# Ragged self-attention on one core: another order of the work ahead of the loops

## The chip, the cores and the metric

The kernel runs on one core of one Trainium2 chip. The metric is the device time of one execution in microseconds (us), taken as the median of several runs. Times inside an execution are counted from the start of the profiled span.

## What is computed

For each of 32 batch entries `b`, the first `lengths[b]` rows of `x[b]` (up to 512 rows of 512 numbers) are projected to queries, keys and values by `w_qkv`, split into 8 heads of 64, and attention is computed within those rows. The other rows of the output are zero.

```
qkv = x_b @ w_qkv;  q, k, v = split(qkv)        # x_b: (seq_len, 512)
scores = q @ k.T / sqrt(64)                     # per head
out_b = softmax(scores) @ v                     # rows past seq_len stay zero
```

`x` is (32, 512, 512) in fp32, `w_qkv` (512, 1536) in fp32; the lengths are drawn between 64 and 511.

## The kernel before, in words

The kernel computes in f16 and accumulates in fp32. It sorts the 32 entries by length on the chip, longest first, and then runs twelve loops (`LOOPS`, L202), one for each width from 512 down to 96. One pass of a loop handles two entries ("positions" 0 and 1). How often each loop runs depends on the lengths: the loop ends are counted on the chip into the tile `ends_i` and are read from there into registers of each of the five engines.

The order of the instructions on each engine is written out by hand. In a loop it stands in the strings of `ORDER` (L204): `S` is a pair of score matmuls with the exponential on ACT (L981, L995), `Q`, `K`, `V` project a part of the *next* entry (matmuls at L228 and L239, copies from PSUM at L1023 and L1039), `A` multiplies by the values and divides (L1065 to L1086), `X` transposes the next input by DMA. So while one entry's attention is computed, the next entry is projected, and the entry after it is loaded and cast. Semaphore waits are worked out by `plan_waits` from what each step reads and writes; they don't change the order.

The change is in `before_loops` (L296), the part ahead of the first loop. It is a list of steps; each engine executes its own steps in the order of that list. In the kernel before it goes like this:

- SP starts the loads of `lengths` (`row`) and of the value weights `w_v` in two halves (L342, L343), ACT starts `col`. POOL makes indices and constants, among them `ones` (L352), 32 partitions by 128.
- DVE makes a sort key for each entry, `least` (L399) is the smallest key, which names the longest entry. Ranks come from comparisons, and two matmuls on PE (`phit_i` and `phit_l`, L446) spread the sorted order and lengths over all partitions (`order`, `slen`).
- SP waits for `least` (`n0`, L538), and then starts the load of the longest entry `x0` in four tiles x0.0 to x0.3 (L540), the query and key weights `w_q` and `w_k` in two halves each (L541 to L544), and, once the order is read (`n1`), `x1` in two halves (L546). All of them are on SP's queue.
- PE runs `warm` (L551), 24 matmuls of the identity that nothing reads, behind the two matmuls of the sort.
- DVE works out the loop ends: `more`, `counts`, `shifted`, `ends_f`, `ends` (L555 to L592), and then casts x0.0 to f16.
- ACT casts the four parts of `w_v` (`shorten`, L679), then x0.1; DVE casts x0.0 and x0.2, POOL x0.3 (`cast_tile`). `turn` (L640) transposes a cast tile on PE (L645) and copies it to `xT0` (L654): below, t00 to t03 are the transposes of x0 and T00 to T03 their copies. `step` (L661) projects: V0 to V3 with `values` (L239), Q0 to Q3 and K0 to K3 with `project` (L228), each followed by a copy from its PSUM bank (L677) on DVE or ACT.
- `read_ends` (L594) loads the three words of `ends_i` into registers of one engine (three loads at L600, with shifts and masks behind each, L606 and L607). DVE does it behind the copy of V2, ACT behind that of V3, POOL and PE amid the query and key steps, SP at the end.
- x1 is cast in four tiles (POOL, DVE, POOL, ACT), and its four transposes stand on PE between K2 and K3. K0 writes PSUM bank 1, which Q2 used before it; K1 writes bank 2, K2 bank 0, the transposes of x1 banks 3 to 6, K3 bank 7.
- Behind that stand the cast of the third entry on POOL (`C`), the first DMA transposes, and empty steps (`joinPE` and others, L815), which make an engine wait for what it needs before the loops.

A program prints the functions that the diff touches, and what calls them, with the line numbers of the profile:

Of the kernel before, what the change touches and what calls it, by code (L numbers as in the profile page):

```python
# [14 lines left out]
ALU = mybir.AluOpType  # L15
AX = mybir.AxisListType

P = 128
# [130 lines left out]
def kernel(  # L149
# [8 lines left out]
    nc = tc.nc  # L158
    B, MAXS, D = x.shape
    NT = MAXS // P  # L160
# [9 lines left out]
    w_q = const.tile([P, NC, D], FP32)  # L170
    w_k = const.tile([P, NC, D], FP32)
# [121 lines left out]
    def of(handles, e):  # L293
        return next(h for h in handles.handles if h.engine == EN[e].engine)

    def before_loops():  # L296
# [35 lines left out]
        def weights(name, tile_, m0, c0, c1):  # L332
            op(
                f"{name}{c0}",
                "SP",
                lambda: sp.dma_start(out=tile_[:, c0:c1, :], in_=w_in[:, c0:c1, m0 : m0 + D]),
                (),
                [f"{name}.{c}" for c in range(c0, c1)],
                dma=True,
            )  # L340
# [11 lines left out]
        ones16 = small("ones", "POOL", lambda t: pool.memset(t, 1.0), shape=(B, P), dtype=F16)  # L352
        limits = small("limits", "POOL", iota([[-32, COUNTS], [0, B // 2]], 0, 448), (), (P, COUNTS, B // 2), I32)
        blank = small("blank", "POOL", lambda t: pool.memset(t, 0.0), shape=(P, P))
        ident = small(
            "ident",
            "POOL",
# [156 lines left out]
            op(name, "SP", load, ("order",))  # L514

        def fetch(name, b, at, k, t0, t1):
            op(
                name,
                "SP",
                lambda: sp.dma_start(  # L520
                    out=x_bufs[b][:, t0:t1, :],
                    in_=xv[bass.ds(found[at][k], 1), :, t0:t1, :].rearrange("o p t d -> (o p) t d"),
                ),
                (),
                [f"xn{b}", *(f"xn{b}.{t}" for t in range(t0, t1))]
                if t1 - t0 == NT
                else [f"xn{b}.{t}" for t in range(t0, t1)],
                dma=True,
            )

        def longest():
            first = nc.alloc_registers("first", engines=[mybir.EngineType.SP])
            reg = of(first, "SP")
            sp.reg_load(reg, least[0:1, 0:1])
            sp.reg_alu(reg, reg, B - 1, op=ALU.bitwise_and)
            found[0] = [nc.snap(first, min_val=0, max_val=B - 1, donate=True)]
# [12 lines left out]
        def warm():  # L549
            for k in range(WARM):  # L550
                nc.tensor.matmul(banks[3][:, 0:P], ident16, ident16, start=True, stop=True)  # L551

        op("warm", "PE", warm, ("ident16",), ("bk3",))

        more = small(  # L555
            "more",
            "DVE",
            lambda t: dve.tensor_tensor(
                out=t,
                in0=slen.rearrange("p (j two) -> p j two", two=2)[:, :, 0]  # L560
                .unsqueeze(1)
                .broadcast_to([P, COUNTS, B // 2]),
                in1=limits,
                op=ALU.is_gt,
            ),
            ("slen", "limits"),
            (P, COUNTS, B // 2),
        )
        counts = small(
            "counts",  # L570
            "DVE",
            lambda t: dve.tensor_reduce(out=t, in_=more, axis=AX.X, op=ALU.add),
            ("more",),
            (P, COUNTS),
        )
        shifted = small(
            "shifted",
            "DVE",
            lambda t: dve.tensor_tensor(out=t, in0=counts, in1=shifts, op=ALU.mult),
            ("counts", "shifts"),  # L580
            (P, COUNTS),
        )
        ends_f = small(
            "ends_f",
            "DVE",
            lambda t: dve.tensor_reduce(
                out=t, in_=shifted.rearrange("p (g k) -> p g k", k=4), axis=AX.X, op=ALU.add
            ),
            ("shifted",),
            (P, COUNTS // 4),  # L590
        )
        op("ends", "DVE", lambda: dve.tensor_copy(out=ends_i, in_=ends_f), ("ends_f",), ("ends",))  # L592

        def read_ends(e, part=None):  # L594
            def load():
                eng = EN[e]
# [82 lines left out]
        for c in range(NC):  # L679
            shorten("wv", w_v, 2 * D, c, "ACT")  # L680

        cast_tile(0, 0, "DVE")
        def joined(name, low, high, bits, after, out=None):

# [12 lines left out]
        def twos(source):  # L697
# [6 lines left out]
        turn(0, 0, "bk4", "DVE")  # L704
        turn(0, 1, "bk5", "ACT")
        cast_tile(0, 2, "DVE")
        cast_tile(0, 3, "POOL")
        step("V0", "bk0", "DVE")
        turn(0, 2, "bk6", "DVE")
        shorten("wq", w_q, 0, 0, "ACT")  # L710
        step("V1", "bk1", "DVE")
        turn(0, 3, "bk3", "ACT")
        shorten("wq", w_q, 0, 1, "POOL")
        op(
            "alive",
            "DVE",
# [19 lines left out]
            (P, B // 2),  # L736
        )
        joined("table", four, computed, 20, ("four", "computed"), table)
        step("V2", "bk4", "DVE")
        shorten("wq", w_q, 0, 2, "ACT")  # L740
        op(
            "M",
            "DVE",
# [24 lines left out]
        shorten("wk", w_k, D, 2, "POOL")  # L768
# [24 lines left out]
        read_ends("SP")  # L793


# [16 lines left out]
        fetch("LD1", 0, 1, 3, 0, NT)  # L812


        op("joinPE", "PE", lambda: None, [f"xT1.{t}" for t in range(NT)], [f"bk{k}" for k in range(3, 7)])  # L815
# [549 lines left out]
```

## Time and profile before

| | |
|---|---|
| median of 3 runs | 345.8 us (345.48, 345.8, 346.64) |
| the profiled execution | 345.26 us |
| its span in the profile | 343.4 us |
| granted TensorE clock, mean | 0.992 |
| first score matmul of the first loop | 22.73 us after the start of the span |

The span is the part of the execution that the profile shows; 1.9 us of the profiled execution lie around it. PE is TensorE with its matmuls, PEld its weight loads, DVE is VectorE, ACT ScalarE, POOL GpSimd, SP SyncE; a q behind a name (SPq, ACTq) means an instruction of the engine's sequencer, such as the start of a DMA or a load of a register, which is not counted as busy time. In the lines of the timeline the columns are start, duration, engine, line, operation, what it writes and reads, and the count; in brackets stands how long the engine had been idle before, and what ended that.

### The profile page before, as it was taken

The numbers are of one execution on the slowest core, as the hardware profiler recorded it, in microseconds if no ns is written. First come the engines' busy times: TensorE is split into PE (matmuls) and PEld (weight loads), VectorE is DVE, ScalarE is ACT, GpSimd is POOL, SyncE is SP. The second block draws the span as 40 slices with busy tenths as digits, with TensorE's granted clock in tenths as the row PEclk, the third lists the DMA queues.
The fourth block names the chain that finished last, engine by engine and source line by source line (L and its number), as shares of the span: only waits on it lengthen the run. The fifth ranks groups of instructions, "written<-read, shape, count | busy, mean of one in ns | idle before, by whom it ended". The sixth has DMA issues, their size and how long they took to land.

```text
span 343.4 us, 10664 instructions
## 1 busy us (share of the span) xinstructions
PE 326.6 (95%) x3846; PEld 201.4 (59%) x3846; DVE 215.3 (63%) x657; ACT 262.7 (77%) x410; POOL 97.9 (29%) x124
## 2 busy tenths in 40 slices
PE   4999999999999999999999999999999999999971
PEld 3444545464555555556655656675677776777751
DVE  6556666667667565465555566677775547777664
ACT  4369899797877878889888898777567788678741
POOL 5466040404030330331133033113222342242311
PEclk9999999999999999999999999999999999999996
DMA  6975974483638936957849549869986656669742
GB/s 224 369 239 131 334 170 135 146 282 90 223 67 287 304 83 226 283 177 285 271 139 307 195 152 338 248 241 238 266 244 198 171 168 216 207 171 238 229 142 79
DMA packets 76060, 73.07 MB, mean 213 GB/s; under 512 B 45808, under 2 KB 45808, under 8 KB 76016
## 3 DMA queue, kind: packets, MB, share of 16 engines
q1 hardware_dynamic: 75968, 72.51, 72.4%
q8 instruction: 24, 0.39, 0.5%
q14 instruction: 20, 0.16, 0.2%
q10 hardware_dynamic: 48, 0.00, 0.0%
HBM read 28.32 MB, written 33.55 MB: 180 GB/s over the span
## 4 chain that ended last, share of the span: by engine, by line
PE 89%; DVE 3%; DMA 2%; issue 1%; SPq 1%; ACT 1%; DVEq 1%; POOL 0%; POOLq 0%
PE banks L228 36%; PE banks L239 21%; PE banks L1065 17%; PE banks L981 15%; DMA out_dram<-out_nat 1%; DVE out_nat L1086 1%; DMA x_nat<-in_x_dram 1%; SPq L255 1%; DVE rcp L1078 1%; DVE qz L677 1%; PE banks L645 1%; DVE v_aug L1039 0%; DVEq L600 0%; DVE rcp L1075 0%; DVE v_aug L677 0%
## 5 line engine op out<-in xcount | busy, mean ns | idle before, releaser
L995 ACT ACTIVATE et<-banks 128x704 f16<-128x704 f32 (+6 forms) x264 | 195.9, 813 | 37.6 <-PE banks L981 36.5
L285 POOL TENSOR_TENSOR x<-x_nat,mask 128x512 f16<-128x512 f32 x87 | 88.3, 1039 | 233.6 <-DVE mask L874 218.3
L228 PE MATMUL banks<-xT,w_r 128*128 128x352 f16 (+11 forms) x1024 | 146.5, 288 | 1.5 <-ACT qz L1023 0.6
L228 PEld LDWEIGHTS banks<-xT,w_r 128*128 128x128 f16 x1024 | 85.0, 98 | 41.6 <-issue 8.7
L239 PE MATMUL banks<-w_r,xT 128*128 128x512 f16 x332 | 85.2, 382 | 0.4 <-ACT xT L654 0.2
L1065 PEld LDWEIGHTS banks<-v_aug,et 128*128 128x128 f16 x1792 | 66.2, 98 | 22.6 <-issue 7.7
L1065 PE MATMUL banks<-v_aug,et 128*128 128x65 f16 x1792 | 74.3, 194 | 1.0 <-ACT et L995 0.7
L1086 DVE TENSOR_TENSOR out_nat<-banks,rcp 128x256 f32<-128x256 f32 (+1 forms) x136 | 64.1, 472 | 5.9 <-DMA out_dram<-out_nat 1.3
L981 PE MATMUL banks<-qz,kT 64*128 64x352 f16 (+11 forms) x640 | 61.6, 298 | 2.8 <-DVE out_nat L1086 1.8
L1075 DVE RECIPROCAL rcp<-banks 128x4 f32<-128x4 f32 (+1 forms) x136 | 25.1, 185 | 44.4 <-PE banks L1065 43.2
L1039 DVE CAST v_aug<-banks 128x512 f16<-128x512 f32 x58 | 40.1, 692 | 18.4 <-PE banks L239 18.2
L239 PEld LDWEIGHTS banks<-w_r,xT 128*128 128x128 f16 x332 | 28.3, 98 | 30.9 <-issue 4.6
L981 PEld LDWEIGHTS banks<-qz,kT 64*128 64x128 f16 x640 | 23.1, 94 | 34.0 <-issue 26.0
L1023 DVE CAST qz<-banks 128x352 f16<-128x352 f32 (+4 forms) x39 | 22.8, 586 | 27.4 <-PE banks L228 27.4
L1023 ACT CAST kT<-banks 128x352 f16<-128x352 f32 (+4 forms) x55 | 26.8, 488 | 13.7 <-PE banks L228 12.8
L1078 DVE TENSOR_TENSOR rcp<-rcp,v_aug 128x4 f32<-128x4 f32 (+1 forms) x136 | 26.1, 192 | 4.7
L1023 ACT CAST qz<-banks 128x320 f16<-128x320 f32 (+5 forms) x52 | 24.5, 477 | 4.9 <-PE banks L228 3.6
L1023 DVE CAST kT<-banks 128x320 f16<-128x320 f32 (+4 forms) x36 | 19.9, 556 | 8.2 <-PE banks L228 7.3
L1039 ACT CAST v_aug<-banks 128x512 f16<-128x512 f32 x21 | 12.5, 596 | 6.1 <-PE banks L239 5.8
L874 DVE TENSOR_SCALAR mask<-alive 128x4 f32 x32 | 5.9, 184 | 5.9 <-issue 5.9
L950 DVE TENSOR_SCALAR v_aug<-alive 128x24 f16 (+3 forms) x32 | 7.2, 224 | 0.0
L446 PE MATMUL banks<-h_hit_i,h_ones 32*128 32x32 f16 x1 | 0.2, 203 | 4.7 <-DVE h_hit_i L429 4.7
(68 smaller groups left out, 48.9 us busy)
## 6 DMA issues: line engine op xcount, KB each, us to landing
x_nat<-in_x_dram SPq DMA_DIRECT2D x12, 768.0 KB, 5.6
out_dram<-out_nat SPq DMA_DIRECT2D x12, 768.0 KB, 4.0
x_nat<-in_x_dram SPq DMA_DIRECT2D x14, 512.0 KB, 4.0
x_nat<-in_x_dram SPq DMA_DIRECT2D x7, 1024.0 KB, 6.7
out_dram<-zeros SPq DMA_DIRECT2D x12, 512.0 KB, 5.4
out_dram<-out_nat SPq DMA_DIRECT2D x12, 512.0 KB, 3.0
out_dram<-out_nat SPq DMA_DIRECT2D x4, 1024.0 KB, 4.7
out_dram<-zeros SPq DMA_DIRECT2D x12, 256.0 KB, 5.4
```

The lines of the kernel that those rows point to most:

```text
L228: last = nc.tensor.matmul(dst[:, 0:N], w_r[:, c, w0 : w0 + P], xT[:, c, 0:N], start=(c == 0), stop=(c == NC - 1),)
L239: last = nc.tensor.matmul(pv, xT[:, c, t * P : (t + 1) * P], w_r[:, c, 2 * D : 3 * D], start=(c == 0), stop=(c == NC - 1),)
L285: return engine.tensor_tensor(out=x16, in0=x32, in1=live.broadcast_to([P, D]), op=ALU.mult)
L950: return nc.vector.tensor_scalar(out=v_bufs[o][:, 0:n, :, HD], in0=alive[:, bass.ds(at("DVE") + (j + 1), 1), 0:n] .rearrange("p o t -> p ( ...
L981: last = nc.tensor.matmul(psc[par][:, x * n128 : x * n128 + N], kT[r, i, kt * P : (kt + 1) * P], qz[r, i, 0:N], start=True, stop=True,)
L995: return nc.scalar.activation(out=et[:, :, x0:x1, 0:N], in_=got.rearrange("p j (x q) -> p j x q", q=n128)[:, :, x0:x1, 0:N], func=AF.Exp, ...
L1023: return copy_on(act)(out=buf[:, ms, 0:N], in_=bank[:, 0 : gm * N].rearrange("p (m q) -> p m q", q=N),)
L1039: return copy_on(act)(out=v_bufs[o][:, t, :, 0:HD], in_=bank.rearrange("p (h d) -> p h d", d=HD))
L1065: last = nc.tensor.matmul(pav[:, g, qt, :], e_bufs[e][:, c0 + qt * P : c0 + (qt + 1) * P], v_aug[:, kt, h, :], start=(kt == 0), stop=(kt = ...
L1075: return nc.vector.reciprocal(out=rcp, in_=pav[:, :, :, HD])
L1078: return nc.vector.tensor_tensor(out=rcp, in0=rcp, in1=v_aug[:, 0:n, h0 : h0 + heads, HD].rearrange("p t g -> p g t"), op=ALU.mult,)
L1086: return nc.vector.tensor_tensor(out=o_t[:, 0:n, h0 * HD : (h0 + heads) * HD].rearrange("p t (g d) -> p g t d", d=HD), in0=pav[:, :, :, 0:HD],
```

## The change

All of it is in `before_loops`; the loops are the same, line for line.

- x0.1 and x0.3 are started by ACT, which first waits for `least` and reads the entry's number itself (`n0a`); x0.0 and x0.2 stay on SP's queue. Nine increments of the semaphore `passed` (`spaced`) stand ahead of that on ACT. ACT's load of its function table, which stood behind the start of `col`, now stands behind these two DMAs.
- `warm0`, 24 matmuls of `ones` by itself (32 partitions, 128 by 128), stands on PE ahead of the two matmuls of the sort. `warm` stays.
- On DVE `shifted`, `ends_f` and `ends` move from ahead of the cast of x0.0 to behind the cast of x0.2; `more` and `counts` stay ahead of it.
- The reads of the three words are spread. ACT reads two of them behind T01 and ahead of its casts of `w_q`, the third behind the copy of V3. DVE reads one behind the copy of V2, one behind Q0's and one behind Q2's; PE one behind each of Q1, Q2 and Q3; POOL one ahead of its casts of `w_q`, one behind, one behind its casts of `w_k`.
- The copy of Q1 goes from DVE to ACT, that of K3 from ACT to DVE. x1 is cast by DVE, ACT, POOL, DVE. POOL casts part 1 of `w_k` ahead of part 2.
- K0 writes bank 3, K1 bank 4, K2 bank 5, K3 bank 7 as before; the transposes of x1 write banks 0, 1, 2 and 6. They stand on PE between K1 and K2, in the order of tiles 0, 1, 3, 2.

```diff
+        def spaced(e, count):
+            def pad():
+                for _ in range(count):
+                    EN[e].sem_inc(passed, 1)
+            op(f"spaced{e}{len(ops)}", e, pad)
...
+        spaced("ACT", 9)
         weights("wv", w_v, 2 * D, 0, NC // 2)
...
+        op(
+            "warm0",
+            "PE",
+            lambda: [
+                nc.tensor.matmul(banks[3][:, 0:P], ones16, ones16, start=True, stop=True)
+                for _ in range(WARM)
+            ][-1],
+            ("ones",),
+            ("bk3",),
+        )
...
         def fetch(name, b, at, k, t0, t1):
+            queue = "ACT" if at == "ACT" else "SP"
             op(
                 name,
-                "SP",
-                lambda: sp.dma_start(
+                queue,
+                lambda: EN[queue].dma_start(
...
-        op("n0", "SP", longest, ("least",))
+        op("n0", "SP", lambda: longest("SP", 0), ("least",))
+        op("n0a", "ACT", lambda: longest("ACT", "ACT"), ("least",))
         for t in range(NT):
-            fetch(f"x0.{t}", 0, 0, 0, t, t + 1)
+            fetch(f"x0.{t}", 0, "ACT" if t % 2 else 0, 0, t, t + 1)
...
         turn(0, 0, "bk4", "DVE")
         turn(0, 1, "bk5", "ACT")
         cast_tile(0, 2, "DVE")
+        shifted = small(
+        ends_f = small(
+        op("ends", "DVE", lambda: dve.tensor_copy(out=ends_i, in_=ends_f), ("ends_f",), ("ends",))
         cast_tile(0, 3, "POOL")
         step("V0", "bk0", "DVE")
         turn(0, 2, "bk6", "DVE")
+        step("V1", "bk1", "DVE")
+        read_ends("ACT", 0)
+        read_ends("ACT", 1)
         shorten("wq", w_q, 0, 0, "ACT")
-        step("V1", "bk1", "DVE")
         turn(0, 3, "bk3", "ACT")
+        shorten("wq", w_q, 0, 2, "ACT")
+        read_ends("POOL", 0)
         shorten("wq", w_q, 0, 1, "POOL")
+        shorten("wq", w_q, 0, 3, "POOL")
+        read_ends("POOL", 1)
+        step("V2", "bk4", "DVE")
+        read_ends("DVE", 0)
...
-        read_ends("DVE")
         step("V3", "bk5", "ACT")
-        read_ends("ACT")
-        shorten("wq", w_q, 0, 3, "POOL")
+        read_ends("ACT", 2)
...
         step("Q0", "bk2", "DVE")
         fetch("x2", 0, 1, 1, 0, NT)
-        shorten("wk", w_k, D, 1, "POOL")
-        step("Q1", "bk0", "DVE")
+        read_ends("DVE", 1)
+        step("Q1", "bk0", "ACT")
         read_ends("PE", 0)
+        shorten("wk", w_k, D, 2, "POOL")
         shorten("wk", w_k, D, 3, "ACT")
         step("Q2", "bk1", "DVE")
-        read_ends("POOL")
-        cast_tile(1, 0, "POOL")
+        read_ends("PE", 1)
+        read_ends("DVE", 2)
+        read_ends("POOL", 2)
+        step("Q3", "bk6", "ACT")
+        read_ends("PE", 2)
+        cast_tile(1, 0, "DVE")
+        cast_tile(1, 1, "ACT")
         cast_tile(1, 2, "POOL")
-        step("Q3", "bk6", "ACT")
-        read_ends("PE", 1)
-        read_ends("PE", 2)
-        cast_tile(1, 1, "DVE")
-        step("K0", "bk1", "DVE")
-        cast_tile(1, 3, "ACT")
-        step("K1", "bk2", "ACT")
-        step("K2", "bk0", "DVE")
-        for t, (bank, eng) in enumerate(
-            (("bk3", "DVE"), ("bk4", "ACT"), ("bk5", "DVE"), ("bk6", "ACT"))
-        ):
+        cast_tile(1, 3, "DVE")
+        step("K0", "bk3", "DVE")
+        step("K1", "bk4", "ACT")
+        for t, bank, eng in ((0, "bk0", "DVE"), (1, "bk1", "ACT"), (3, "bk2", "ACT"), (2, "bk6", "DVE")):
             turn(1, t, bank, eng)
-        step("K3", "bk7", "ACT")
+        step("K2", "bk5", "DVE")
+        step("K3", "bk7", "DVE")
         read_ends("SP")
```

More of the change, by code (lines that the diff above doesn't have):

```diff
@@ L553, in before_loops @@
         op("warm", "PE", warm, ("ident16",), ("bk3",))
[L555 to L592, printed above, removed]
         def read_ends(e, part=None):
@@ L680, in before_loops @@
             shorten("wv", w_v, 2 * D, c, "ACT")
+        more = small(
+            "more",
+            "DVE",
+            lambda t: dve.tensor_tensor(
+                out=t,
+                in0=slen.rearrange("p (j two) -> p j two", two=2)[:, :, 0]
+                .unsqueeze(1)
+                .broadcast_to([P, COUNTS, B // 2]),
+                in1=limits,
+                op=ALU.is_gt,
+            ),
+            ("slen", "limits"),
+            (P, COUNTS, B // 2),
+        )
+        counts = small(
+            "counts",
+            "DVE",
+            lambda t: dve.tensor_reduce(out=t, in_=more, axis=AX.X, op=ALU.add),
+            ("more",),
+            (P, COUNTS),
+        )
         cast_tile(0, 0, "DVE")
@@ L706, in before_loops @@
         cast_tile(0, 2, "DVE")
+        shifted = small(
+            "shifted",
+            "DVE",
+            lambda t: dve.tensor_tensor(out=t, in0=counts, in1=shifts, op=ALU.mult),
+            ("counts", "shifts"),
+            (P, COUNTS),
+        )
+        ends_f = small(
+            "ends_f",
+            "DVE",
+            lambda t: dve.tensor_reduce(
+                out=t, in_=shifted.rearrange("p (g k) -> p g k", k=4), axis=AX.X, op=ALU.add
+            ),
+            ("shifted",),
+            (P, COUNTS // 4),
+        )
+        op("ends", "DVE", lambda: dve.tensor_copy(out=ends_i, in_=ends_f), ("ends_f",), ("ends",))
         cast_tile(0, 3, "POOL")
@@ L812, in before_loops @@
         fetch("LD1", 0, 1, 3, 0, NT)
-        op("joinPE", "PE", lambda: None, [f"xT1.{t}" for t in range(NT)], [f"bk{k}" for k in range(3, 7)])
+        op("joinPE", "PE", lambda: None, [f"xT1.{t}" for t in range(NT)], [f"bk{k}" for k in (0, 1, 2, 6)])
         op("joinACT", "ACT", lambda: None, [f"et{e}" for e in range(4)])
```

16 lines of the change are left out of this document (7 added, 9 removed).

## The prediction

> **What bounds the kernel now.** I read the page first: busy time, and the chain of work that ended last.
>
> ```profile
> PE 326.6 (95%) x3846; PEld 201.4 (59%) x3846; DVE 215.3 (63%) x657; ACT 262.7 (77%) x410; POOL 97.9 (29%) x124
> ...
> PE 89%; DVE 3%; DMA 2%; issue 1%; SPq 1%; ACT 1%; DVEq 1%; POOL 0%; POOLq 0%
> ```
>
> PE carries the chain nearly everywhere, and the loops are the same before and after. So the change is worth as much as it moves the start of the first loop. The second view is PE's timeline ahead of it.
>
> ```profile
> 5.08 2.74 PE L551 MATMUL banks<-h_ident 128*128 128x128 f16 x24
> ...
> 8.57 0.61 PE L645 MATMUL banks<-h_ident,x 128*128 128x128 f16 x4 [0.18 <-ACT x L284]
> 8.97 1.74 PE L239 MATMUL banks<-w_r,xT 128*128 128x512 f16 x4
> 10.55 0.39 PE L645 MATMUL banks<-h_ident,x 128*128 128x128 f16 x4
> 10.78 1.03 PE L239 MATMUL banks<-w_r,xT 128*128 128x512 f16 x4
> 11.64 0.39 PE L645 MATMUL banks<-h_ident,x 128*128 128x128 f16 x4
> 11.87 1.03 PE L239 MATMUL banks<-w_r,xT 128*128 128x512 f16 x4
> 13.12 1.04 PE L239 MATMUL banks<-w_r,xT 128*128 128x512 f16 x4 [0.23 <-ACT xT L654]
> 14.03 3.61 PE L228 MATMUL banks<-xT,w_r 128*128 128x512 f16 x16
> 18.12 2.76 PE L228 MATMUL banks<-xT,w_r 128*128 128x512 f16 x12 [0.47 <-DVE qz L677]
> 20.72 1.06 PE L645 MATMUL banks<-h_ident,x 128*128 128x128 f16 x16
> 21.61 1.03 PE L228 MATMUL banks<-xT,w_r 128*128 128x512 f16 x4
> 22.73 1.07 PE L981 MATMUL banks<-qz,kT 64*128 64x512 f16 x6
> ```
>
> In order: the warming matmuls, t01, V0 to V3 with t02 and t03 between them, Q0 to Q3 from 14.03, K0 to K2 from 18.12, the transposes of x1, K3, the first scores at 22.73. The four matmuls of V0 take 1.74, those of V1 1.03: PE's pace doubled at about 10.4. From 14.03 on PE stands still only for the 0.47 ahead of K0. So three numbers make the start of the loops: when Q0 starts, how long it is from there to K0, and from K0 to the scores. ACT shows what releases Q0.
>
> ```profile
> 1.60 1.28 ACT L622 ACT_TABLE_LOAD   x1 [1.60 <-SPq L1264]
> 5.25 1.14 ACT L622 CAST w_r<-w_v 128x512 f16<-128x512 f32 x2 [2.37 <-DMA w_v<-in_w_qkv_dram]
> 6.57 1.14 ACT L622 CAST w_r<-w_v 128x512 f16<-128x512 f32 x2 [0.18 <-DMA w_v<-in_w_qkv_dram]
> 7.80 0.72 ACT L284 ACTIVATE x<-x_nat,mask 128x512 f16<-128x512 f32 x1
> 9.22 0.58 ACT L654 COPY xT<-banks 128x512 f16<-128x512 f16 x1 [0.70 <-PE banks L645]
> 11.96 0.62 ACT L622 CAST w_r<-w_q 128x512 f16<-128x512 f32 x1 [2.16 <-DMA w_q<-in_w_qkv_dram]
> 12.48 0.58 ACT L654 COPY xT<-banks 128x512 f16<-128x512 f16 x1
> 13.27 0.62 ACT L622 CAST w_r<-w_q 128x512 f16<-128x512 f32 x1 [0.20 <-DMA w_q<-in_w_qkv_dram]
> ...
> 22.68 0.58 ACT L677 CAST kT<-banks 128x512 f16<-128x512 f32 x1 [0.24 <-PE banks L228]
> ```
>
> The second half of `w_q` lands at 13.27, its cast ends at 13.89, and V3 leaves PE at the same time: Q0 is bound by a DMA and by PE at once. ACT idles for 2.16 ahead of that, waiting for the first half.
>
> **When Q0 starts after the change.** Four things move here.
>
> ```profile
> 1.41 0.94 SPq L336 DMA_DIRECT2D w_v<-in_w_qkv_dram  x2
> ...
> 1.69 0.19 POOL L352 MEMSET h_ones<- 32x128 f16 x1
> ...
> 3.47 0.17 DVE L402 TENSOR_REDUCE h_least<-h_key_row 32x1 int32<-32x32 f32 x1
> ...
> 4.48 1.94 SPq L520 DMA_DIRECT2D x_nat<-in_x_dram  x4
> ```
>
> *The second queue.* SP starts four tiles in 1.94, the first 0.84 after `least` is there (3.64 to 4.48). With ACT doing the same beside it, two each, x0.3 is started about 0.95 earlier, and `w_q` and `w_k` too. That helps only if the DMA engines were short of work, and they were not:
>
> ```profile
> 6.00:8.00 2.00, 2.00 (x21) 1.77 (x19) 1.79 (x11) 1.73 (x4) 2.00 (x8) 1.00 1.06 360
> 8.00:10.00 2.00, 1.82 (x11) 0.99 (x10) 1.01 (x3) 1.10 (x2) 0.80 (x5) 1.00 0.80 243
> ```
>
> In these stretches the last two columns are the DMA share and GB/s: 1.06 and 360, then 0.80 and 243 with `w_q` and `w_k` already started. What is slow from 8 to 10 is the reading of x0, not its issue. So I leave the landings of `w_q`, `w_k` and x1 where they are; were the slow stretch gone, some (360-243) x 2 = 234 KB, or 0.65 at 360 GB/s, would be won on them. What the second queue does change is the order: x0.1 and x0.3 don't stand behind the rest of `w_v` any more, and x0.0 and x0.2 give way to them. The Trainium skill, in "DMA: Bandwidth & Descriptors", section "Queues, rings and completion order", says that each DMA engine goes round between the queue rows that have work, packet by packet. No run here shows two loading queues; by that rule x0.2 would be the last of the four, and the sum below would take its late end.
>
> ```profile
> 6.52 0.17 DVE L579 TENSOR_TENSOR h_shifted<-h_counts,shifts 128x12 f32<-128x12 f32 x1
> ...
> 7.19 0.54 DVE L280 TENSOR_SCALAR x<-x_nat,mask 128x512 f16<-128x512 f32 x1
> ...
> 9.33 0.49 DVE L280 TENSOR_SCALAR x<-x_nat,mask 128x512 f16<-128x512 f32 x1 [0.47 <-DMA x_nat<-in_x_dram]
> ...
> 16.18 1.89 DVE L677 CAST qz<-banks 128x512 f16<-128x512 f32 x3 [2.10 <-issue]
> ```
> ```profile
> 10.43 1.04 POOL L285 TENSOR_TENSOR x<-x_nat,mask 128x512 f16<-128x512 f32 x1 [1.62 <-DMA x_nat<-in_x_dram]
> ...
> 16.05 1.17 POOL L622 CAST w_r<-w_k 128x512 f16<-128x512 f32 x2 [0.71 <-DMA w_k<-in_w_qkv_dram]
> 18.93 2.04 POOL L285 TENSOR_TENSOR x<-x_nat,mask 128x512 f16<-128x512 f32 x2 [1.70 <-issue]
> ```
>
> Before, x0.2 landed at 9.33 and x0.3, the last, at 10.43. After it, x0.2 lands between 8.6 (no slow stretch) and 10.4 (last of the four); I take the middle of the two rows, 9.9.
>
> *The table load.* Before, its 1.28 lay under the wait for `w_v`. Now ACT waits for `least`, issues two DMAs (0.97 by half of SP's four) until about 5.45, loads the table until 6.7, casts `w_v` until 9.0 (before 7.7) and x0.1 until 9.7 (before 8.5). The nine increments lie under the wait for `least` and cost nothing; without that cover I can't price them from a row. T01 ends near 10.7 instead of 9.8.
>
> *The clock.* `ones` is there at 1.88, and 24 matmuls at L551's 2.74 end at about 4.7, when the sort's first matmul wants PE (4.74 in the first wait's end): nothing to 0.1 lost. PE's pace doubled 5.3 after L551 began, so it now may double at about 7.3. V0 then takes 1.03 instead of 1.74, which pays for its later start (10.0 instead of 9.0): V0 to V2 end within 0.2 of before.
>
> *The loop ends.* Moving three short operations off DVE (6.52 to 7.19) frees x0.0's cast at 6.5, but x0.0 has to land first; worth nothing. But `ends` now comes after x0.2: cast 0.49, three operations 0.67. Two of ACT's reads wait for it, and ACT's casts of `w_q` and T03 are queued behind them:
>
> ```profile
> L600 DVEq TENSOR_LOAD <-ends_i x3: 302/315/551, 12.9 to 15.2; - x3
> L600 ACTq TENSOR_LOAD <-ends_i x3: 275/280/504, 14.2 to 15.8; - x3
> ```
>
> (First and last start at the end.) A read with its shifts is 0.8 on ACT, half of 14.2 to 15.8. So: x0.2 at 9.9, `ends` at 11.05, reads until 12.65, cast 0.62, T03 0.58, cast 0.62, less 0.2 of overlap: 14.3, and with the 0.14 that lie before between the cast's end (13.89) and Q0 it starts at 14.45. **Term 1: +0.4.** With x0.2 at 8.6 the reads start with T01's copy, the casts are done at 13.6, and PE's V3 sets Q0 at about 13.75: -0.3. With x0.2 at 10.4 it is 14.95, and 15.1 with a T01 late as well: +1.1.
>
> **From Q0 to K0.** Before, K0 waits for bank 1, that is for Q2's copy, and DVE came to the copies of Q0 to Q2 only at 16.18: three reads in a row, 12.9 to 15.2 for the starts, are the 2.10 of "issue". After, K0 writes bank 3, which T03 left long ago, each read on DVE stands behind another copy, and one copy has gone to ACT. PE's own three reads lie under its 16 matmuls, as before. The stall goes, 0.47, or 0.63 with the overlap that streaming matmuls have (16.18 + 1.89 ends at 18.07, and 14.03 + 3.61 less 0.16 of drain is 17.48). What is late next is `w_k`: its last casts end at 17.22 on POOL, after it 0.6 sooner by the other order, so nothing binds unless Q0 comes before 13.7. **Term 2: -0.55.**
>
> **From K0 to the scores.** The same 32 matmul steps. x1's casts end at 20.97 on POOL (18.93 + 2.04); after, POOL has one tile, so the last cast ends near 19.7, before t12 wants it. The loop's entry no longer waits for x1's copies, which gains up to 0.25 (21.61 + 1.03 less 0.16 to 22.73). But the third pair of scores needs K3's copy, which lay on ACT until 23.26 (22.68 + 0.58) and is on DVE now, at 0.63 or more (1.89 for three). So the gain at the first pair is given back at the third. **Term 3: 0**, between -0.25 and +0.1.
>
> **Sum.** +0.4 - 0.55 + 0 = -0.15 on the profiled execution's 345.26 (span 343.4 and 1.9 around it): 345.1. That execution is 0.5 below the median of the runs shown, 345.8, and they spread over 1.16. **Term 4** is in the median: where PE's pace doubles later than at 10.4, V1 and t03 pay (1.74 for 1.03, 0.61 for 0.39), 0.9 in all, straight ahead of Q0. With the early matmuls no execution pays it: 0 to -0.9, I take -0.3 for the median. 345.8 - 0.15 - 0.3 = **345.3**. The Trainium skill, "TensorE: Matmul & The Clock Gate", Part 1, has the clock rise after one busy window of some 3.4 us that runs free of the kernel's start. By that the rise differs from execution to execution, which is term 4; the 5.3 here fits it.
>
> **Rivals.**
> - *Faster.* x0 flows without the slow stretch, x0.2 lands by 8.6, ACT's reads are done before `w_q` lands: -0.3 - 0.6 - 0.25 = -1.15, and term 4: 344.35. For it: the reads of 8 to 10 are slow with one queue only; against: the share was 0.80 and the tiles are the same.
> - *Slower.* The two reads on ACT take the place of DVE's three. From x0.2 at 10.05 on (Q0 at 14.6) they cost more than the stall that went, and each 0.1 later is 0.1 more: at 10.4 with a late T01, +1.1 - 0.47 + 0.1 = +0.73: 346.5, without term 4. For it: the order of the two queues; against: DMA may finish all four sooner.
> - *It does not do what it says.* Matmuls of 32 partitions don't raise the clock. Then V0's late start isn't paid for: 0.7 more on V3, Q0 at 15.1, 346.3. L551's 24 still come.
>
> **Chances.** Forecast (344.8 to 346.0) 0.5; faster rival 0.22; term 4 in full, 345.8 - 0.15 - 0.9 = 344.75, 0.06; slower rival 0.17; no warming 0.05. 0.3% of 345.8 is 1.04, about what a measurement can tell from no change. Faster by more takes the faster rival or term 4 in full: 0.27. Slower by more (over 346.84) takes the slower rival past x0.2 at 10.7: 0.11. Within it 0.62. The range runs from 344.0, the faster rival with a little more of term 4, to 346.5.
>
> **What would show it.** PE's row of V0 at about 1.03; ACT's table load at 5.5; `ends` later than 10; Q0 between 13.75 and 15.1; no wait of K0 for a copy on DVE; the first scores at 22.1 to 22.9. The prediction is wrong if `w_q` lands well before 13, if PE waits for x1's transposes, or if anything in the loops moves by more than the start did.

## The result, and the profile after

The changed kernel takes 347.7 us, the median of 19 runs (346.6 to 349.74), against 345.75 of the kernel before in as many runs (345.13 to 346.93). The ratio is 1.0059, with a 95% interval of 1.0042 to 1.0075: slower, by 2.0 us. The profiled execution of the changed kernel took 347.57, its span is 345.7. One run of all that follow, 379.75 in e12 at a granted clock of 0.852, is a slow one and is left out of its ratio.

Busy time and the head of the chain of waits, from the page of the changed kernel:

```profile
PE 330.0 (95%) x3870; PEld 204.6 (59%) x3870; DVE 217.2 (63%) x658; ACT 262.2 (76%) x410; POOL 96.9 (28%) x123
...
PE 89%; DVE 3%; issue 2%; SPq 2%; ACT 1%; DMA 1%; POOL 0%; ACTq 0%; POOLq 0%; DVEq 0%
```

PE is still the bound; "issue" and SPq have grown from 1% to 2% each. PE's timeline ahead of the loops, after the change:

```profile
1.93 2.74 PE L369 MATMUL banks<-h_ones 32*128 32x128 f16 x24 [1.93 <-POOL h_ones L362]
...
4.92 2.74 PE L573 MATMUL banks<-h_ident 128*128 128x128 f16 x24
8.38 0.61 PE L627 MATMUL banks<-h_ident,x 128*128 128x128 f16 x4 [0.72 <-DVE x L280]
9.33 0.61 PE L627 MATMUL banks<-h_ident,x 128*128 128x128 f16 x4 [0.34 <-ACT x L284]
9.73 1.91 PE L239 MATMUL banks<-w_r,xT 128*128 128x512 f16 x4
11.43 0.63 PE L627 MATMUL banks<-h_ident,x 128*128 128x128 f16 x4
11.86 1.91 PE L239 MATMUL banks<-w_r,xT 128*128 128x512 f16 x4
13.57 0.54 PE L627 MATMUL banks<-h_ident,x 128*128 128x128 f16 x4
13.95 1.89 PE L239 MATMUL banks<-w_r,xT 128*128 128x512 f16 x8
15.67 5.40 PE L228 MATMUL banks<-xT,w_r 128*128 128x512 f16 x24
20.91 1.06 PE L627 MATMUL banks<-h_ident,x 128*128 128x128 f16 x16
21.80 1.89 PE L228 MATMUL banks<-xT,w_r 128*128 128x512 f16 x8
23.63 0.61 PE L1006 MATMUL banks<-qz,kT 64*128 64x512 f16 x4
24.57 0.39 PE L1006 MATMUL banks<-qz,kT 64*128 64x512 f16 x2 [0.34 <-DVE kT L659]
```

V0 (9.73) and V1 (11.86) take 1.91 each: PE is at half pace until 13.9, although warm0 (1.93) and warm (4.92) kept it busy from 1.93 to 7.66. Q0 starts at 15.67. From there to K0 nothing is waited for any more (24 matmuls in one piece), and the third pair of scores waits 0.34 for K3's copy on DVE. ACT and DVE show what comes late around it, first ACT:

```profile
4.24 0.90 ACTq L541 DMA_DIRECT2D x_nat<-in_x_dram  x2
5.17 1.28 ACT L604 ACT_TABLE_LOAD   x1 [5.17 <-DVE order_i L479]
6.47 2.18 ACT L604 CAST w_r<-w_v 128x512 f16<-128x512 f32 x4
8.55 0.72 ACT L284 ACTIVATE x<-x_nat,mask 128x512 f16<-128x512 f32 x1
9.97 0.58 ACT L636 COPY xT<-banks 128x512 f16<-128x512 f16 x1 [0.70 <-PE banks L627]
13.19 0.62 ACT L604 CAST w_r<-w_q 128x512 f16<-128x512 f32 x1 [2.63 <-DVE xT L636]
14.15 0.58 ACT L636 COPY xT<-banks 128x512 f16<-128x512 f16 x1 [0.34 <-PE banks L627]
```

and DVE:

```profile
7.77 0.56 DVE L280 TENSOR_SCALAR x<-x_nat,mask 128x512 f16<-128x512 f32 x1 [1.20 <-DMA x_nat<-in_x_dram]
...
10.10 1.17 DVE L280 TENSOR_SCALAR x<-x_nat,mask 128x512 f16<-128x512 f32 x1 [0.65 <-DMA x_nat<-in_x_dram]
...
11.59 0.17 DVE L727 CAST ends_i<-h_ends_f 128x3 int32<-128x3 f32 x1
```

x0.0 lands at 7.77 (before, its cast started at 7.19). The cast of x0.2 takes 1.17, not the 0.49 of before, `ends` is written at 11.76, and the 2.63 that ACT idles ahead of its first cast of `w_q` are its two reads of the loop ends and the wait for them. What came last ahead of Q0, though, is PE: the copy T03 (14.15) stands 0.34 for the transpose t03, behind V1 at half pace, when the reads (done at 13.15) and the cast behind them are over. V0 in turn stands behind t01, which waits 0.34 for ACT's cast of x0.1 (8.55, before 7.80), behind the table load and the casts of `w_v`.

Then comes something that has nothing to do with the start. The same stretch of PE's timeline in the loops, first before, then after:

```profile
241.93 0.71 PE L1065 MATMUL banks<-v_aug,et 128*128 128x65 f16 x18
242.84 1.89 PE L239 MATMUL banks<-w_r,xT 128*128 128x512 f16 x8 [0.20 <-issue]
```
```profile
243.00 0.71 PE L1090 MATMUL banks<-v_aug,et 128*128 128x65 f16 x18
245.09 1.89 PE L239 MATMUL banks<-w_r,xT 128*128 128x512 f16 x8 [1.39 <-issue]
```

This is the entry to the loop of width 256, whose first step on PE is V0. PE stands for 1.39 instead of 0.20, and what ended it is "issue": nothing that the profile shows. In the trace PE's sequencer takes the branch into the loop, and its next instruction comes 1.29 later; before, it came 0.13 later. Below this is called **the stop**.

How far PE is behind its own place in the kernel before, step by step:

| step | before | after | later by |
|---|---|---|---|
| V0 | 8.97 | 9.73 | 0.76 |
| Q0 | 14.03 | 15.67 | 1.64 |
| K0 | 18.12 | 19.19 | 1.07 |
| first scores | 22.73 | 23.63 | 0.90 |
| third pair of scores | 23.41 | 24.57 | 1.16 |
| V0 of the loop of width 256 | 242.84 | 245.09 | 2.25 |
| first scores of the loop of width 96 | 332.32 | 334.36 | 2.04 |

Between these rows the shift stays within 0.2, but for the stretch ahead of the last one, of which more below. So in PE's timeline the loss has two parts of about the same size: some 1.0 at the start, 1.2 at the stop.

### The profile page after: what moved, and what is told of

Its sections match the earlier page's. It is cut to its first block, busy times and chain, and to the rows that moved or that the text cites. A ratio compares the mean times of both kernels' runs of the same rounds, so it can differ in the third digit from the quotient of the medians.

```text
span 345.7 us, 10726 instructions
## 1 busy us (share of the span) xinstructions
PE 330.0 (95%) x3870; PEld 204.6 (59%) x3870; DVE 217.2 (63%) x658; ACT 262.2 (76%) x410; POOL 96.9 (28%) x123
## 4 chain that ended last, share of the span: by engine, by line
PE 89%; DVE 3%; issue 2%; SPq 2%; ACT 1%; DMA 1%; POOL 0%; ACTq 0%; POOLq 0%; DVEq 0%
PE banks L228 36%; PE banks L239 21%; PE banks L1090 17%; PE banks L1006 15%; SPq L255 1%; DVE out_nat L1111 1%; DVE rcp L1103 1%; PE banks L627 1%; DMA out_dram<-out_nat 1%; ACT w_r L604 0%; DVE v_aug L1064 0%; ACT L604 0%; ACTq L541 0%; DVE rcp L1100 0%; DVE kT L659 0%
## 5 line engine op out<-in xcount | busy, mean ns | idle before, releaser
L285 POOL TENSOR_TENSOR x<-x_nat,mask 128x512 f16<-128x512 f32 x86 | 87.3, 1039 | 237.7 <-DVE mask L899 220.6
L899 DVE TENSOR_SCALAR mask<-alive 128x4 f32 x32 | 6.9, 216 | 5.8 <-issue 5.8
L975 DVE TENSOR_SCALAR v_aug<-alive 128x24 f16 (+3 forms) x32 | 8.4, 263 | 0.0
```

The lines of the kernel that those rows point to most:

```text
L285: return engine.tensor_tensor(out=x16, in0=x32, in1=live.broadcast_to([P, D]), op=ALU.mult)
L975: return nc.vector.tensor_scalar(out=v_bufs[o][:, 0:n, :, HD], in0=alive[:, bass.ds(at("DVE") + (j + 1), 1), 0:n] .rearrange("p o t -> p ( ...
```

## The experiments

At first I held these theories: the stop comes from the place of PE's code, which the 24 matmuls of warm0 push further ("place"), against another part of the change as its cause; and at the start the two reads on ACT, the second queue and the clock share the loss. In all of the runs below the ratio is to the kernel before on the same chip, with its 95% interval, and one matmul counts as two instructions (it has a weight load).

**e1: without warm0.** The op `warm0` is left out.

> The changed kernel without warm0, all else kept. Theory of place: PE's stop of 1.2 at the entry to the loop of width 256 comes from its code, which the 24 matmuls push further; without them the stop is gone (next instruction 0.1 after the branch) and the time is 347.7 - 1.2 = 346.5, with the first scores where they were (23.6), since warm0 did not raise the clock (it rose at 13.9 with it). Rival 1: the stop belongs to another part of the change; it stays, and the time is 347.7. Rival 2: warm0 does help the clock in the median, whatever one profile shows; without it V1 and t03 are later by up to 0.9 and the time is up to 348.6.

Measured: 346.82, ratio 1.0015 (0.9992 to 1.0038). The stop is gone (0.13 from the branch to the next instruction), the first scores are at 23.44. The clock rose at 13.54, with warm0 at 13.88. Place and "warm0 does nothing for the clock" hold; rival 2 falls.

**e2: the kernel before with warm0 alone.**

```diff
+        op(
+            "warm0",
+            "PE",
+            lambda: [
+                nc.tensor.matmul(banks[3][:, 0:P], ones16, ones16, start=True, stop=True)
+                for _ in range(WARM)
+            ][-1],
...
```

> The kernel before with warm0 alone added. Theory of place: the stop at the entry to the loop of width 256 appears here too, 1.2, and nothing else changes: 345.75 + 1.2 = 346.95, first scores at 22.7. Rival (the prediction's): the clock rises at about 7.3 and V0 takes 1.03; the start is bound by the load of w_q all the same, so 345.5 to 345.75 and no stop.

```profile
241.79 0.71 PE L1075 MATMUL banks<-v_aug,et 128*128 128x65 f16 x18
243.87 1.89 PE L239 MATMUL banks<-w_r,xT 128*128 128x512 f16 x8 [1.36 <-issue]
```

PE's timeline of e2 has the stop, 1.36, in a kernel that is otherwise the one before. The time isn't 1.2 more, though: 346.1, ratio 1.0006 (0.9989 to 1.0023). In the profile the start is 0.15 earlier, and of the 2.07 that PE is behind at the loop of width 128, 1.24 are made good ahead of the loop of width 96. So the stop is there as expected, and the sum around it was not.

**e3: warm0 on 128 partitions.**

```diff
-        ones16 = small("ones", "POOL", lambda t: pool.memset(t, 1.0), shape=(B, P), dtype=F16)
+        ones16 = small("ones", "POOL", lambda t: pool.memset(t, 1.0), shape=(P, P), dtype=F16)
```

> The changed kernel with ones on 128 partitions, so that warm0's matmuls fill the whole array instead of 32 rows. If the clock counts rows in use: it rises by 10.5 or earlier, V0 or V1 take 1.03, T03 no longer waits for t03 (0.34), Q0 starts 0.4 earlier, 347.3. If 24 matmuls more ahead of the sort do nothing for the clock whatever their rows: V0 and V1 at 1.9 each, the rise near 13.9 or wherever its own phase puts it, 347.7. The stop at the loop of width 256 stays in both.

```profile
1.93 2.74 PE L369 MATMUL banks<-h_ones 128*128 128x128 f16 x24 [1.93 <-POOL h_ones L362]
...
4.93 1.83 PE L573 MATMUL banks<-h_ident 128*128 128x128 f16 x24
9.30 1.04 PE L627 MATMUL banks<-h_ident,x 128*128 128x128 f16 x8 [2.54 <-DVE x L280]
10.43 1.89 PE L239 MATMUL banks<-w_r,xT 128*128 128x512 f16 x4
12.11 0.56 PE L627 MATMUL banks<-h_ident,x 128*128 128x128 f16 x4
12.50 1.03 PE L239 MATMUL banks<-w_r,xT 128*128 128x512 f16 x4
```

Now the clock rises amid warm: its 24 matmuls take 1.83 instead of 2.74. By the trace's record of the clock it rose at 5.62, fell at 9.04 and rose again at 12.45, because PE then paused 2.54 for x0.0. So rows in use count, and in this execution the gain was lost in the pause. The time is 347.64, ratio 1.0042 (1.0026 to 1.0059); the profiled execution is the slowest of its eight, 350.01, 2.1 above the next.

**e4: all of x0 on SP's queue.** `n0a` and the nine increments are left out.

> The changed kernel with all four tiles of x0 on SP's queue; ACT neither waits for least nor starts loads, and the nine increments are gone too. Theory that ACT's queue of work ahead of Q0 is the bound: table load and casts of w_v back to where they were before (casts done at 7.7), V0 at 9.0, x0.2 at 9.4 and ends at 10.7, ACT's two reads done by 12.2, T03 by 13.2, V3 until 14.2: Q0 at 14.2 to 14.5, 1.2 to 1.4 earlier; the stop at width 256 stays: 346.4. Rival: the reads that wait for ends set Q0 alone and ends stays near 11.7, since DVE's cast of x0.2 takes 1.2 beside POOL's: Q0 within 0.4 of 15.7, 347.4 to 347.7.

Measured: 346.37, ratio 1.0000 (0.9982 to 1.0017). V0 starts at 8.93 and takes 1.04, Q0 starts at 14.59, the first scores at 22.50 (after: 23.63). The first theory holds: 1.1 of the start go with the second queue and what it does to ACT, 0.80 of them at V0 already. The clock was up at 8.41 here and not at 13.88, so V0 and V1 ran at full pace too; V2 and V3 then wait 0.55 and 0.80 for T02 and T03, which stands behind ACT's reads. The stop is there.

**e5: e2 with 16 increments of a semaphore ahead of warm0 on PE.**

> The kernel before with warm0 and 16 increments of the semaphore passed ahead of it on PE: PE does the same work as in e2, its code in the loops lies 15 instructions further. Theory of place (the stop depends on where PE's code lies, not on how much stands ahead of it): no stop at the entry to the loop of width 256; clock as early as in e2 (up by 9), so against before -0.15 at the start and up to -0.9 in executions whose clock rises late: 345.1 to 345.8 where before has 346.1, ratio 0.997 to 0.999. Rival: any code added ahead brings the stop, or warm0's matmuls themselves do: gap of 1.4 there, ratio 1.000 to 1.002 as in e2.

Measured: 346.49, ratio 1.0000 (0.9983 to 1.0016). The increments aren't free: warm0 starts at 3.80 instead of 1.93, the sort and x0 follow, and V0 starts at 10.26. So the time tells nothing of the stop. The gap at the stop does: 0.53, neither 0.2 nor 1.4. Place matters, but not as a switch.

**e7: e5 with K0 in bank 3.** (No e6 was run.)

```diff
-        step("K0", "bk1", "DVE")
+        step("K0", "bk3", "DVE")
...
-            (("bk3", "DVE"), ("bk4", "ACT"), ("bk5", "DVE"), ("bk6", "ACT"))
+        for t, bank, eng in ((0, "bk1", "DVE"), (1, "bk4", "ACT"), (3, "bk6", "ACT"), (2, "bk5", "DVE")):
```

> e5 with K0 in bank 3 and the transposes of x1 in banks 1, 4, 6, 5 (tiles 0, 1, 3, 2): the part of the change that takes K0's wait for DVE's copy away, alone. K0's wait of 0.47 goes and the transposes or the third pair of scores give back at most 0.15 of it, since K3's copy stays on ACT: 0.3 to 0.5 below e5, ratio to before 0.996 to 0.998. Rival: w_k's casts or x1's casts on POOL (last one at 20.97 before) become the wait instead, and the third pair of scores starts no earlier than in e5.

Measured: 345.66, ratio 0.9969 (0.9953 to 0.9985), 0.8 below e5. Its 28 matmuls from Q0 to K2 run in one piece, while in e5 K0 waited 0.91. The theory holds, by more than it said, since e5's wait was longer than 0.47.

**e8: the loop ends worked out ahead of x0.0's cast, as before.**

> The changed kernel with shifted, ends_f and ends back ahead of DVE's cast of x0.0; two queues, warm0 and all else kept. If the reads that wait for ends set Q0: ACT reads from 10.6 on, is done by 11.9, casts w_q until 12.5, and waits for t03; with T03 at 13.0 to 14.1 Q0 starts at 14.6 to 15.6, 347.0 or less. If PE's cold V0 and V1 set it (t03 ends at 14.1 whatever ACT does): T03 at 14.15 as before, Q0 within 0.1 of 15.7, 347.7. The stop at the loop of width 256 stays in both.

```profile
12.14 0.62 ACT L604 CAST w_r<-w_q 128x512 f16<-128x512 f32 x1 [1.57 <-DMA w_q<-in_w_qkv_dram]
13.37 0.58 ACT L636 COPY xT<-banks 128x512 f16<-128x512 f16 x1 [0.61 <-PE banks L627]
```

ACT's timeline of e8. Measured: Q0 at 14.89 and the third pair at 23.73, 0.84 earlier than in the changed kernel. The reads are done at 11.35, but this doesn't show that they set Q0: T03 (13.37) waits for t03 here as in the changed kernel, and t03 comes earlier because the clock rose at 12.22, in time for a part of V1, which takes 1.18 instead of 1.91. That is 0.73 of the 0.78 at Q0. But the time isn't lower: 348.87, ratio 1.0070 (1.0045 to 1.0095). In the profiled execution 0.82 of the gain is still there at 300, and then PE waits 1.53 for a transpose on SP's queue at 330.77 and 1.32 for DVE at 339.84. Why the end of this kernel was worse is not settled.

**e9: x0.3 cast by DVE, behind `ends`.**

> The changed kernel with the cast of x0.3 on DVE, behind ends, instead of POOL. If POOL's cast beside it is what slows DVE's cast of x0.2: that takes 0.5 to 0.6 instead of 1.17, ends comes at 11.1 instead of 11.76 and ACT's reads are done by 12.5. Q0 then gains up to 0.5 if the clock happens to rise early, and nothing if V1 is cold (t03 at 13.5): 347.2 to 347.7. Rival: DVE's cast is slow for another reason (the load of x0.3 landing beside it): 1.0 or more again.

```profile
10.37 0.49 DVE L280 TENSOR_SCALAR x<-x_nat,mask 128x512 f16<-128x512 f32 x1 [0.92 <-DMA x_nat<-in_x_dram]
...
11.17 0.17 DVE L727 CAST ends_i<-h_ends_f 128x3 int32<-128x3 f32 x1
```

DVE's timeline of e9: without POOL beside it the cast of x0.2 takes 0.49, and `ends` is there at 11.34. Q0 starts at 15.16, 0.5 earlier; 0.4 of that is V1, which takes 1.51 since the clock rose at 12.83, and T03 again waits for t03, 0.25. The time doesn't show it: 348.12, ratio 1.0054 (1.0031 to 1.0077).

**e10: the kernel before with e7's banks alone.**

> The kernel before with K0 in bank 3 and the transposes of x1 in banks 1, 4, 6, 5 (tiles 0, 1, 3, 2), nothing else: term 2 of the prediction alone, with PE's code where it was. By that term K0's wait of 0.47 goes; the third pair of scores starts 0.3 to 0.5 earlier (22.9 to 23.1), no stop at the loop of width 256, ratio 0.9985 to 0.999. Rival: x1's cast on POOL (ends at 20.97) or the load behind it is next, and nothing is won: ratio 1.000, third pair at 23.4.

Measured: 345.14, ratio 0.9984 (0.9958 to 1.0010). No wait of K0, no stop. As expected in size, though the interval holds 1. In its profiled execution the clock rose late (12.79), so its start can't be compared with that of before row by row.

**e11: e10 with early work in as many matmuls as before.** warm0 is 6 matmuls of 512 columns on 128 partitions, warm is 18 of 160 columns.

> e10 with PE busy from 1.9 on, but with as many matmuls as before: warm0 is 6 matmuls of 512 columns on 128 partitions, warm 18 of 160 columns instead of 24 of 128. Theory of place: as PE's code in the loops lies where it lay before, there is no stop (gap of 0.2 at the loop of width 256), although PE does early work. Theory that the clock counts the array's rows in use over a window: it rises by 8.8 in any phase, V0 and V1 take 1.03. Then 0.15 to 0.9 less than e10: ratio 0.996 to 0.998. Rivals: early work brings the stop wherever the code lies (gap 1.4, ratio about 1.001); the clock falls again in the pause ahead of t00 as in e3 (V0 at 1.9, ratio as e10).

```profile
241.20 0.71 PE L1081 MATMUL banks<-v_aug,et 128*128 128x65 f16 x18
242.11 1.89 PE L240 MATMUL banks<-w_r,xT 128*128 128x512 f16 x8 [0.20 <-issue]
```

No stop, though PE works from 1.93 on. The clock rose at 5.89 and stayed up to 333.57; V0 took 1.03, K0 started 0.75 earlier than before. 345.1, ratio 0.9968 (0.9943 to 0.9994).

**e12: the kernel before with the second queue alone** (`spaced`, `n0a`, and x0.1 and x0.3 started by ACT).

> The kernel before with the second queue alone: nine increments and n0a on ACT, x0.1 and x0.3 started by ACT, no warm0, all else as before. From the traces of the changed kernel and e4: the table load and w_v's casts end 1 later (8.7), x0.1's cast at 9.3, V0 at 9.7; w_q lands 0.4 earlier. If DVE's order of before (ends ahead of x0.0) keeps ACT free, Q0 is bound by V3: two V of 1.9 in the cold put it at 14.4 to 15.0, +0.4 to +1.0; ratio 1.001 to 1.003, no stop. Rival (the faster one of the prediction): the earlier w_q sets Q0, at 13.6: ratio 0.999.

```profile
8.48 0.49 DVE L280 TENSOR_SCALAR x<-x_nat,mask 128x512 f16<-128x512 f32 x1 [1.44 <-DMA x_nat<-in_x_dram]
...
10.38 1.17 DVE L280 TENSOR_SCALAR x<-x_nat,mask 128x512 f16<-128x512 f32 x1 [0.28 <-DMA x_nat<-in_x_dram]
```
```profile
10.16 1.89 PE L239 MATMUL banks<-w_r,xT 128*128 128x512 f16 x4
...
14.95 3.62 PE L228 MATMUL banks<-xT,w_r 128*128 128x512 f16 x16
19.47 2.76 PE L228 MATMUL banks<-xT,w_r 128*128 128x512 f16 x12 [0.91 <-DVE qz L689]
...
24.08 1.07 PE L993 MATMUL banks<-qz,kT 64*128 64x512 f16 x6
```

DVE's and PE's timelines of e12: the casts of x0.0 and x0.2 start at 8.48 and 10.38 (7.19 and 9.33 before), V0 starts at 10.16, Q0 at 14.95, 0.92 later than before, and the first scores at 24.08, 1.35 later, since K0 waits 0.91 instead of 0.47. The shift stays at 1.3 to 1.5 to the end. 347.5, ratio 1.0039 (1.0009 to 1.0069). The rival falls; the loss is larger than I expected.

**e13: the changed kernel without warm0 and without the second queue.**

> The changed kernel without warm0 and with all of x0 on SP's queue: what is left is the moved loop ends, the spread reads, the banks and the order of copies and casts. From e4's trace (Q0 +0.56, K0 -0.06, third pair +0.04 against before) and without its early clock the start is 0 to 0.9 later than before's and there is no stop: ratio 1.000 to 1.002. Rival: the medians add up (changed kernel 1.0059, less 0.0044 for warm0 and 0.0059 for the queue): ratio 0.996, and the rest of the change is worth 1.5.

Measured: 345.75, ratio 0.9988 (0.9969 to 1.0007): between the two. The clock rose at 8.74 here, without warm0; V0 took 1.04. The third pair of scores is 0.27 later than before: the banks' gain is spent by ACT's reads (V3 waits 0.80 for T03) and by K3's copy (0.34).

**e14 and e15: e11's work in more instructions.** warm0 as 24 matmuls of 128 columns (e14) or 12 of 256 (e15), warm as 24 of 128.

> e11 with the same early work in more instructions: warm0 is 24 matmuls of 128 columns instead of 6 of 512 (each some 2.7 in all), warm 24 of 128 columns instead of 18 of 160. PE's code in the loops lies where it lies in the changed kernel. Theory of place: the gap at the entry to the loop of width 256 is back at 1.4, with the same start as e11: 1.2 more, ratio 1.000 to 1.001. Rival: the stop came from 32 partitions, from ones as weights, or from another part of the change, and is not here: gap of 0.2, ratio 0.996 to 0.998.

> As e14, with warm0 as 12 matmuls of 256 columns: PE's code lies half as far on. If the stop is a pause of the sequencer at one fixed place of the code (a page of 256 instructions), which matmuls already queued hide unless it falls on the entry itself: here it falls some 24 instructions behind the entry, amid V0 and V1, gap of 0.2 to 0.3, ratio as e11 (0.996 to 0.998). Rival: the stop grows with the distance, gap of 0.7, ratio 0.998 to 1.000.

```profile
243.46 1.89 PE L240 MATMUL banks<-w_r,xT 128*128 128x512 f16 x8 [1.35 <-issue]
```
```profile
242.10 1.89 PE L240 MATMUL banks<-w_r,xT 128*128 128x512 f16 x8 [0.23 <-issue]
```

PE's timelines of e14, then e15. The stop is back in e14 and not in e15: e14 345.78, ratio 0.9985 (0.9959 to 1.0011); e15 344.85, ratio 0.9978 (0.9949 to 1.0007). With all 16 kernels the place theory is shown for the gap, and the rival that the stop grows with the distance falls:

| PE's code in the loops lies further by | kernels | branch to next instruction | gap ahead of V0 |
|---|---|---|---|
| 0 or 1 | before, e1, e10 to e13 | 0.13 | 0.2 |
| 25 | e15 | 0.12 | 0.23 |
| 48 or 49 | after, e2, e3, e4, e8, e9, e14 | 1.29 | 1.35 to 1.39 |
| 63 or 64 | e5, e7 | 0.42, 0.35 | 0.53, 0.45 |

Of all these kernels only e7 and e11 have a ratio whose interval lies wholly below 1.

## Why the prediction was wrong, point by point

- **"... the loops are the same before and after. So the change is worth as much as it moves the start of the first loop."** This is the step that failed for 1.19 of the 2.25 that PE is behind at V0 of the loop of width 256. The loops are the same line for line, but PE's code for them lies 49 instructions further, and at one loop entry that costs 1.19. The prediction priced warm0 at "nothing to 0.1 lost", by what it delays; what it shifts was not a term. By its own sentence it was to be wrong if anything in the loops moved by more than the start did, and that is what happened.
- **Term 1, Q0 at 14.45.** It is 15.67, 1.22 later, and here the wait was wrong. The sum lets ACT's reads release Q0. They are late: `ends` comes 0.7 later than in the sum, since DVE's cast of x0.2 takes 1.17 beside POOL's cast of x0.3 (e9 has 0.49 without it), and the reads end 0.5 later (13.15 for 12.65). But T03 then still waits 0.34 for t03: PE came last, with V0 and V1 at half pace, though V0 itself starts at 9.73, ahead of the forecast 10.0. Behind T03 the sum was short as well: it ended with the cast of `w_q`, 0.42 and 0.14 behind T03, where V3 stands behind T03 too, with 0.94 to Q0, 0.38 more. In e4 and e13, with PE at full pace, the reads do bind.
- **The clock.** "... so it now may double at about 7.3": it doubled at 13.9. The rival *it does not do what it says* had the mechanism: 24 matmuls of 32 partitions don't raise it. With them the clock rose at 8.4 to 13.9 (after, e2, e4, e5, e7, e8, e9), without them at 8.7 to 13.5 (before, e1, e10, e12, e13), with 128 partitions at 5.6 to 7.9 (e3, e11, e14, e15). "... which pays for its later start" therefore failed, in this execution: from V0 to Q0 PE takes 5.94, before 5.06. Each of these rises is that of one execution. They differ in something else too: in the six profiles with the second queue (after, e1, e3, e8, e9, e12) the last rise ahead of the loops lies at 12.0 to 13.9, in the ten others at 5.9 to 12.8, and PE pauses 0.7 to 2.5 for x0.0 in the six. That this pause holds the rise back fits e3, but no run tested it alone.
- **The second queue.** "What the second queue does change is the order" was right, and x0.2 at 9.9 too (10.10). But the delay of x0.0 was left without a price, and in e12 that is the dear one: 1.3 on x0.0, 1.35 on the first scores. Over the profiles x0.0's cast starts at 7.77 to 8.75 with two queues (six of them) and at 7.12 to 7.53 with one (eight, without e5 and e7, whose sort comes later). The Trainium skill says in "DMA: Bandwidth & Descriptors", section "Issuing engines are not separate DMA queues", that starting DMAs on several engines saves only the sequencer's time. The trace agrees: the last tile of x0 came at 10.43 on one queue (before) and at 10.38 on two (e12).
- **Term 2, -0.55.** The shift falls from 1.64 at Q0 to 1.07 at K0: -0.57. Right, and the wait is gone in e7 and e10 too.
- **Term 3, 0.** -0.17 at the first pair, +0.09 at the third, with the wait for K3's copy that it named. Right.
- **Term 4, -0.3.** Not to be seen in the changed kernel, whose clock rises no earlier. What an early rise is worth stays open: e11 and e15 have V0 to V2 at 1.03, and Q0 at 13.80 and 13.76 (before, 14.03), but e11's ratio lies within e10's interval.

How much each part is worth in the times is less sure than in PE's timeline. Without the second queue the ratio is lower by 0.59% (changed kernel and e4), 0.39% (e12 and before) and 0.27% (e1 and e13). Without the 24 matmuls more, and with them the stop, it is lower by 0.44% (changed kernel and e1), 0.12% (e4 and e13), 0.07% (e14 and e15) and 0.06% (e2 and before). Each of these differences is uncertain by 0.2 to 0.4%. So the times show the second queue's price in two of three pairs, and the stop's in one of four, the one with the changed kernel itself; the 1.19 is a figure of the traces, and e2 shows how a later wait can take it back.

What stays open: why PE's sequencer pauses there. The page of the changed kernel lists the loads of code:

```profile
q8 instruction: 24, 0.39, 0.5%
```

24 packets of 16 KB. In the kernel before PE starts 1010 instructions from the packet at 227.20 to the fourth after it at 266.44, so some 250 for each. The Trainium skill, "Runtime: NRT & Kernel Launch", section "Instruction fetch mechanics", says that code comes in blocks of 256 instructions and that crossing from one to the next is mostly hidden. That the stop is such a crossing that falls on the entry, where no matmuls are queued to hide it, fits the table (with 25 it would fall amid V0 and V1, and the stop vanishes), but no run showed it. No such packet runs during the stop in the seven kernels with the gap of 1.35 or more: in the changed kernel they start at 238.01 and 246.84, and the stop lies from 243.5 to 244.8.

## What to carry to other kernels

Work put ahead of loops also moves the code of the loops: compare the gaps at every loop entry before and after, and when one has grown with "issue" as its reason, change the number of instructions ahead, not the loop. The second queue didn't bring the set of tiles sooner here; it brought the first of them later, so ask which tile the chain waits for. Warming matmuls on 32 partitions did nothing that the clock's record shows, on 128 they raised the clock; they need work behind them soon enough that the clock doesn't fall again.

## What the runs showed of the hardware

- The clock is decided in windows of 3.41 that run free of the kernel's start: in e3 its three changes lie 3.41 apart, and over the 16 profiles the first rise lies anywhere from 5.6 to 13.9. The Trainium skill, "TensorE: Matmul & The Clock Gate", Part 1, has that window, and counts it as busy or idle. Here a window with little but 32-partition matmuls in its first third (3.64 to 7.06 of the changed kernel, worked back from the rise at 13.88) didn't count as busy, though PE never stood still in it. In e4 the window from 1.59 to 5.00, the one ahead of the rise at 8.41, held them and the sort's two from 1.94 on, and the clock stayed down.
- DVE's cast of 128x512 takes 0.49 alone and 1.17 when POOL casts beside it (after, e12): in the changed kernel it began at 10.10 and ended at 11.27, 0.28 after POOL's, which ended at 10.99.
- An increment of a semaphore on PE costs 0.15: those of e5 stand 0.15 apart, from 1.58 to 3.69, and moved warm0 from 1.93 to 3.80.
- The packets above, taken for loads of PE's code, meet the DMA transposes. In ten kernels (before, after, e1 to e9) a transpose during which such a packet (0.9 to 1.8 long) ran took 1.80 on the mean (110 of them), the others 1.31 (700). Where they meet depends on the place of the code, and so does the end of the kernel. In each of the ten kernels whose code lies 25 or more further, PE waits 1.0 to 1.6 for a transpose in the loop of width 128; in the six others it waits 1.1 to 1.9 for DVE instead, ahead of the scores of the loop of width 96. In the changed kernel, PE's and SP's timelines:

```profile
331.14 1.96 PE L228 MATMUL banks<-xT,w_r 128*128 128x128 f16 x32 [1.08 <-SPq L259]
```
```profile
326.48 3.43 SPq L255 DMA_TRANSPOSE xT<-x  x2
```

  Two transposes take 3.43 there, 2.51 at the same place before. The two waits are about equal, which is why the shift ends at 2.04 and not above. That the packets cause the long transposes is argued from their meeting, not shown.
- A wait of that length can also cost the clock. In e10's profiled execution PE waited 1.73 at 333.09, the clock fell at 333.64 for one window, and the 32 matmuls that follow took 2.72 instead of 1.52 (before). In e11 it fell so at 333.57, after a wait of 1.93 at 332.18; waits of 1.45 in e12 and e13 cost nothing of it.
